# Shift, scale and gate vectors of a two-layer model: strips of columns on TensorE in place of GpSimd sums

## Chip, cores and metric

One core of a Trainium2 chip runs the whole forward pass in one launch. The metric is device time in microseconds (us) of that launch, the lower the better. The kernel before takes 1464.41 us (median of 3 runs, 1463.18 to 1467.83).

## The reference, cut to what matters

Two layers over 256 tokens of 1024 features in float32. Each layer's two sublayers are modulated by vectors that come from one conditioning vector `c` (1 x 1024) and a large matrix:

```python
def ada(c, w, b, n):
    m = jax.nn.silu(c) @ w + b
    return [t[:, None, :] for t in jnp.split(m, n, axis=-1)]
...
for i in range(DEPTH):
    sh1, sc1, g1, sh2, sc2, g2 = ada(c, ada_w[i], ada_b[i], 6)
    h = modulate(rmsnorm(x, norm_mix[i]), sh1, sc1)
    ...                       # layer 0: gMLP; layer 1: attention with its own kv shift and scale
    x = x + g1 * y
    h = modulate(rmsnorm(x, norm_ffn[i]), sh2, sc2)
    x = x + g2 * moe(...)     # 64 experts, 8 of them per token, and a shared one
```

`ada_w[i]` is 1024 x 6144 and `kv_ada_w` 1024 x 2048. So 56 MB of matrices are multiplied by one vector each, a product of one row. All other matrix products have 256 rows or the rows that the router gives an expert.

## The kernel before, in words

**Blocks.** Every weight is loaded by SP's queue in blocks of 1 MB, 128 partitions x 2048 float32, into slots of 1 MB (9 in the first and third stage, 14 in the expert stages). A block of a modulation matrix holds 256 of its columns: `w[:, k, :]` for k = 0..7 is rows 128k to 128k+127. There are 24 such blocks for each layer (`a` and `A`) and 8 for the attention's keys and values (`k`), 56 in all.

**One block's sum** (class `Sum`, lines 312 to 361). The eight parts are scaled by the silu of `c` (`cs[:, k]`, one number a partition) and added into `w[:, 0, :]`. Then `total` (line 344) adds over the partitions with two TensorE matmuls against a column of ones, and `close` adds the bias. The slot is free after `total`. There are two modes. Mode `v`: VectorE does it all, one TENSOR_SCALAR and seven SCALAR_TENSOR_TENSOR, each 128x256. Mode `q`: ScalarE scales the parts in eight ACTIVATEs, and GpSimd adds them in three TENSOR_TENSORs of 1024, 512 and 256 columns.

**Stages.** (1) The start, lines 1139 to 1199: blocks 0 to 7 of layer 0 are summed (`QUIET` names the two in mode `q`), the tokens are normalized and modulated, and the first matmul of the gMLP follows. (2) The gMLP loop, lines 1297 to 1327, 48 steps: 16 `Tok` and 16 `Feat` steps of 24 matmuls each, then 16 `Out` steps. Each step's weights are split into a high and a low float32r part three steps ahead: ScalarE copies (`high`), VectorE subtracts (`low`), and in steps 16 to 43 every fourth `low` is GpSimd's (`split`, line 488, `turns`). (3) The expert stage of layer 0, `moe` from line 609: residual, router, order of the experts, then 56 blocks of expert rows in `run`. (4) The attention loop, lines 1510 to 1546, 32 steps, whose pairs of heads pass through VectorE, ScalarE, GpSimd and TensorE. (5) The expert stage of layer 1.

**What sets the order.** From line 1214 on every engine runs its instructions in the order of the program. Into the two loops the sums are dealt out by hand. `BEGIN` and `BEGIN1` (lines 42, 49) name the step in which a block's sum begins; `lighter` (line 525) chooses its mode; and `tick` (line 508), at the end of each step, gives each engine a budget of estimated microseconds (`BUDGET`, `BUDGET1`, lines 43, 55) and issues operations from the open sums until it is spent. A sum that is done waits until its age in steps passes 2; then `finish` issues its `total`. `flush` finishes what a later stage needs. `pump`, `settle` and `rest` (lines 529 to 551, 1333) do the same around the router. Modulation blocks k5 to k7 are summed there, and A0 among the experts (line 1073).

Of the kernel before, what the change touches and what calls it, by code (L numbers as in the profile page):

```python
# [16 lines left out]
P = 128  # L17
# [15 lines left out]

QUIET = (2, 5)


# [5 lines left out]
BEGIN = [(4 + 2 * i, x) for i, x in enumerate(ITEMS) if 4 + 2 * i < 46]  # L42
BUDGET = ((1.0, 1.2, 2.5), (1.6, 1.2, 2.5), (0.6, 1.2, 2.5))

# [9 lines left out]
QUEUE1 = [x for _, x in QUEUE1] + [("s", 0)]  # L54
BUDGET1 = ((1.3, 1.2, 2.5),) * 3 + ((0.8, 0.2, 2),) + ((1.8, 1.6, 3.4),) * 2 + ((1.4, 1.5, 2.5),) * 2

# [123 lines left out]
def tile_model(ctx: ExitStack, tc: tile.TileContext, A: dict, out: bass.AP):  # L180
# [3 lines left out]
    class Ordered:  # L184


        def __init__(self, eng):
            self.eng = eng
# [42 lines left out]
    def wk(shape=(P, 512), dt=F32):  # L231
        return ps.tile(list(shape), dt, tag="wk", name=nm("wk"), bufs=4)
# [27 lines left out]
    def low(t, src, eng=None):  # L260
        (eng or V).tensor_tensor(t[:, 1], src, t[:, 0], ALU.subtract)
# [21 lines left out]
    onesf = cst.tile([P, P], F32, name="onesf")  # L283
    G.memset(onesf, 1.0)
    ident = cst.tile([P, P], F32, name="ident")
    G.affine_select(ident, onesf, [[-1, P]], ALU.is_equal, 0.0, base=0, channel_multiplier=1)
# [25 lines left out]
    class Sum:  # L312

        def __init__(self, w, biasT, at, dstT, dst=None, mode="v"):
            self.w, self.biasT, self.at, self.dstT, self.dst, self.mode = w, biasT, at, dstT, dst, mode
            self.ops = {V: [], S: [], G: []}
            o = w[:, 0, :]  # L320
            for k in range(KT):
                c = cs[:, k:k + 1]
                if mode == "q":
                    self.add(S, 0.4, lambda k=k, c=c: S.activation(w[:, k, :], w[:, k, :], AF.Copy, scale=c))
                elif k:
                    self.add(V, 0.4, lambda k=k, c=c: V.scalar_tensor_tensor(o, w[:, k, :], c, o, ALU.mult, ALU.add))
                else:
                    self.add(V, 0.4, lambda c=c: V.tensor_scalar(o, o, c, None, ALU.mult))
            for k, t in ((4, 2.3), (2, 1.2), (1, 0.7)) if mode == "q" else ():
                self.add(G, t, lambda k=k: G.tensor_tensor(w[:, 0:k, :], w[:, 0:k, :], w[:, k:2 * k, :], ALU.add))  # L330

# [6 lines left out]
        def begin(self):  # L338
            for e in (V, S, G):
                for _, f in self.ops[e]:  # L340
                    f()
                self.ops[e] = []

        def total(self, pt):

            for q in range(2):
                T.matmul(pt[:, q:q + 1], self.w[:, 0, q * P:(q + 1) * P], onesf[:, 0:1], start=True, stop=True)

# [138 lines left out]

    def split(steps, k, pool, turns=None):


        if k + LA < len(steps):
            f = steps[k + LA]
            f.h = high(f.part(), pool)
        if 0 <= k + LA - 1 < len(steps):
            f = steps[k + LA - 1]
            low(f.h, f.part(), G if turns and k % turns == turns - 1 else V)

# [7 lines left out]

    credit = {V: 0, S: 0, G: 0}

    def tick(tv, ts, tg):

        spread()  # L510
        for f in list(active):
            if not f.left(V, S, G):
                f.age = getattr(f, "age", 0) + 1
                if f.age > 2:
                    f.finish()
                    active.remove(f)
        for e, t in ((V, tv), (S, ts), (G, tg)):
            credit[e] = min(credit[e], 0) + t
            for f in active:
                while credit[e] > 0 and f.ops[e] and not (e is G and f.left(V, S)):  # L520
                    t, op = f.ops[e].pop(0)
                    op()
                    credit[e] -= t

    def lighter():

        return "q" if sum(f.left(S) for f in active) < sum(f.left(V) for f in active) + 0.1 else "v"

    def pump(*engs):

        for e in engs:
            for f in active:
                if not (e is G and f.left(V, S)):
                    for _, op in f.ops[e]:
                        op()
                    f.ops[e] = []

    def settle(n=99):

        fs = [f for f in active if not f.left(V, S, G)][:n]  # L540
        if fs:
            pt = wk((P, 2 * len(fs)))
            for i, f in enumerate(fs):
                f.total(pt[:, 2 * i:2 * i + 2])
                settled.append((f, pt[:, 2 * i:2 * i + 2]))
                active.remove(f)
# [62 lines left out]
    def moe(l, own, rw, first, rest):  # L609
# [41 lines left out]
        early = len(active)  # L651
        pump(G)
        squares(0, 2)
# [4 lines left out]
        squares(1, 3)  # L658
        rest("q")
        pump(S)  # L660
# [19 lines left out]
        for k, eng, b in ((0, V, pr), (4, G, rb)):  # L680
            eng.tensor_tensor(hT[:, k:k + 4, :], xT[:, k:k + 4, :], b.unsqueeze(1).to_broadcast([P, 4, 256]), ALU.mult)

        pump(G)


# [106 lines left out]
        for tt in range(2):  # L792
            T.matmul(pst[:, tt * P:(tt + 1) * P], slot[:, tt, :], identb, start=True, stop=True)
        shared_up(16 - SH1)
        spread()
# [5 lines left out]
        V.tensor_copy(pub, puf)  # L801
        rest(*"vqvqvq")

# [7 lines left out]
        for tt in range(2):  # L811
            V.tensor_scalar(wsel[:, tt, :], wsel[:, tt, :], wrec[:, tt:tt + 1], 2.5, ALU.mult, ALU.mult)
        pump(V, S, G)
        ready = all(f.dst is None for f in active)
# [213 lines left out]
        def run():  # L1028
# [7 lines left out]
            for b in range(nblk + 2):  # L1036
# [36 lines left out]
                while due and due[0][0] <= b:  # L1073
                    begin(due.pop(0)[1], lighter())
                tick(1.6, 1.6, 4.2)
                next(over, None)
# [62 lines left out]
    with phase("pb") as pool:  # L1139
# [25 lines left out]
        for i in range(8):  # L1165
            f = ada(0, i, load(A["wada"][0, i]), "q" if i in QUIET else "v")
            if i == 1:
                nc.sync.dma_start(xt, A["x"].rearrange("(a p) d -> p a d", p=P))
            f.begin()
            f.total(pa[:, 2 * i:2 * i + 2])  # L1170
            if i == 1:
                rt = b8((P, 2, D))
                normed(pieces(xt), rt, rstd_of(pieces(xt), rt))
                pts = transposed(rt, ("acc",) * 4)
# [20 lines left out]
        for q in range(2):  # L1195
            low(early[q], wi[0][:, 4 * q:4 * q + 4, :], G)
        V.tensor_tensor(adaT[0][:, 0:16], pa, pkc("adab0")[:, 0:16], ALU.add)
# [99 lines left out]
        for k in range(n + 16):  # L1297
            for at, x in BEGIN:
                if at == k:
                    begin(x, lighter())  # L1300
            if k in (2, 6, 10):
                fetch_bv(512 * (k + 2) // 4, 512)
            split(steps, k, pool, 4 if 16 <= k < 44 else None)
            e = k + 4 - n
# [20 lines left out]
            if k >= 42:  # L1325
                next(weighing, None)
            tick(*((0, 1.2, 0) if 17 <= k < 20 or k > 45 else BUDGET[k // 16]))
        settle()
# [4 lines left out]
    def rest(*modes):  # L1333

        for x, m in zip(list(sums), modes):
            begin(x, m)
# [300 lines left out]
```

## Time and profile before

| what | value |
|---|---|
| runs, median (lowest to highest) | 1464.41 us (1463.18 to 1467.83) |
| the profiled execution's own time | 1460.32 us |
| its span in the trace | 1458.6 us |
| TensorE matmul, busy | 1352.2 us, 93% |
| VectorE (DVE), busy | 853.3 us, 58% |
| ScalarE (ACT), busy | 537.5 us, 37% |
| GpSimd (POOL), busy | 213.9 us, 15% |
| moved by DMA | 516.59 MB, mean 354 GB/s |
| mean granted clock of TensorE | 0.961 |

The profile is one execution; its records give each instruction's start and length on its engine. PE is TensorE's matmul row, PEld its weight loads. Busy shares are averages over stages with different limits, so the prediction reads them stage by stage. "Idle before" and "waited for" name the engine whose work ended a wait. PEclk is the share of TensorE's full clock that was granted.

### The profile page before, as it was taken

How to read it: one execution, taken by the hardware profiler on the slowest of the kernel's cores; microseconds unless marked ns; L12 is line 12 of the kernel's file. 1: busy time of each engine (PE TensorE's matmuls, PEld its weight loads, DVE VectorE, ACT ScalarE, POOL GpSimd, SP SyncE). 2: the span in 40 equal slices, each digit the busy share in tenths (PEclk: the TensorE clock that was granted, in tenths of full speed). 3: DMA queues.
4: the chain of work that ended last, by engine and by line, in shares of the span. 5: the costliest groups of instructions: out<-in, count | busy, mean ns of one | idle time of the engine just before them, and what ended most of it. 6: DMA issues, size and time to landing. Idle time of an engine off the chain costs nothing. (4 is left out here: it accounts for less than half of the span.)

```text
span 1458.6 us, 27101 instructions
## 1 busy us (share of the span) xinstructions
PE 1352.2 (93%) x10782; PEld 893.6 (61%) x10782; DVE 853.3 (58%) x1568; ACT 537.5 (37%) x1143; POOL 213.9 (15%) x160
## 2 busy tenths in 40 slices
PE   4797888899999999999988988899999999999996
PEld 3797866655555555555547966775555555555553
DVE  7898897544444444444459977854444444444444
ACT  4565556222322222323236656342322223222222
POOL 4135355110000000000004644320000000000000
PEclk7799999899999999999999989999999999999998
DMA  9876767499999999999995855759999999999995
GB/s 371 323 262 230 271 224 314 173 368 418 420 419 419 419 419 419 420 418 420 419 403 210 324 178 207 286 206 390 405 419 419 420 419 419 419 419 420 419 419 216
DMA packets 72697, 516.59 MB, mean 354 GB/s; under 512 B 8308, under 2 KB 8436, under 8 KB 10358
## 3 DMA queue, kind: packets, MB, share of 16 engines
q1 hardware_dynamic: 72132, 514.03, 87.3%
q8 instruction: 86, 1.41, 0.4%
q10 hardware_dynamic: 436, 0.79, 0.2%
q14 instruction: 43, 0.35, 0.1%
HBM read 513.75 MB, written 1.05 MB: 353 GB/s over the span
## 5 line engine op out<-in xcount | busy, mean ns | idle before, releaser
L194 PE MATMUL wk<-w,b 128*32 128x256 f32 (+1 forms) x4928 | 413.2, 386 | 10.7 <-DMA w<-in_wexp_dram 10.7
L194 PEld LDWEIGHTS wk<-w,b 128*32 128x32 f32 (+1 forms) x4928 | 236.2, 122 | 153.5 <-DMA w<-in_wexp_dram 16.3
L194 DVE TENSOR_TENSOR s<-s,s 64x512 fp32r<-64x512 f32 x220 | 151.0, 686 | 125.3 <-ACT s L194 121.8
L194 PE MATMUL wk<-w,ht 128*32 128x512 f32 (+1 forms) x1232 | 212.5, 601 | 0.4 <-ACT ht L194 0.4
L194 DVE TENSOR_TENSOR s<-wk,g 128x512 f32<-128x512 f32 x110 | 76.1, 692 | 185.2 <-PE wk L194 185.2
L194 POOL TENSOR_TENSOR w<-w 128x1024 f32<-128x1024 f32 (+2 forms) x84 | 135.0, 1608 | 183.1 <-ACT w L194 179.4
L194 DVE SCALAR_TENSOR_TENSOR w<-w,cs 128x256 f32<-128x256 f32 x196 | 153.7, 785 | 5.3
L194 PE MATMUL wk<-s,b 128*128 128x256 f32 (+2 forms) x1024 | 149.4, 295 | 0.0
L194 POOL TENSOR_TENSOR t<-t,mhalf 128x2 f32<-128x2 f32 (+1 forms) x7 | 4.6, 662 | 971.7 <-DVE t L194 971.7
L194 ACT COPY ht<-wk 128x128 f32<-128x128 f32 x110 | 29.3, 266 | 312.0 <-PE wk L194 312.0
L194 ACT CAST s<-s 64x512 fp32r<-64x512 f32 x220 | 134.4, 611 | 15.2 <-DVE s L194 12.4
L194 PEld LDWEIGHTS wk<-s,b 128*128 128x128 f32 (+1 forms) x1024 | 124.7, 185 | 15.7 <-issue 1.1
L194 PE MATMUL acc<-s,h 128*128 128x512 f32 x440 | 131.6, 420 | 0.4 <-DVEq L1086 0.4
L194 ACT ACTIVATE b<-wk,adaT,sc 128x256 f32<-128x256 f32 x112 | 63.3, 565 | 180.5 <-DVE b L194 180.5
L194 DVE TENSOR_SCALAR b<-wk,sc,adaT 128x256 f32<-128x256 f32 x112 | 61.0, 544 | 100.5 <-PE wk L194 100.2
L194 ACT ACTIVATE h<-wk 64x256 f32<-64x256 f32 (+1 forms) x114 | 43.0, 378 | 195.0 <-PE wk L194 195.0
L194 PEld LDWEIGHTS wk<-w,ht 128*32 128x32 f32 (+1 forms) x1232 | 50.4, 120 | 94.3 <-issue 89.3
L194 PEld LDWEIGHTS acc<-s,h 128*128 128x128 f32 x440 | 74.0, 188 | 52.7 <-DVE s L194 35.1
L194 DVE TENSOR_TENSOR scr<-w,scr 128x1024 fp32r<-128x1024 f32 x71 | 102.5, 1449 | 5.8 <-ACT scr L194 5.7
L194 DVE SCALAR_TENSOR_TENSOR h<-wk,ws,h 64x256 f32<-64x256 f32 x110 | 54.0, 491 | 80.1 <-ACT h L194 79.3
L194 ACT CAST scr<-w 128x1024 fp32r<-128x1024 f32 x80 | 83.2, 1045 | 45.8 <-PE wk L194 23.2
L194 ACT ACTIVATE w<-w,cs 128x256 f32<-128x256 f32 x224 | 96.6, 502 | 0.9 <-DMA w<-in_wada_dram 0.8
(238 smaller groups left out, 1428.9 us busy)
## 6 DMA issues: line engine op xcount, KB each, us to landing
w<-in_wexp_dram SPq DMA_DIRECT2D x384, 1024.0 KB, 16.7
w<-in_wada_dram SPq DMA_DIRECT2D x48, 1024.0 KB, 8.0
w<-in_win_dram SPq DMA_DIRECT2D x16, 1024.0 KB, 7.1
w<-in_wqkvo_dram SPq DMA_DIRECT2D x16, 1024.0 KB, 8.6
w<-in_wout_dram SPq DMA_DIRECT2D x8, 1024.0 KB, 6.4
w<-in_wkva_dram SPq DMA_DIRECT2D x8, 1024.0 KB, 6.5
w<-in_wsh_dram SPq DMA_DIRECT2D x6, 1024.0 KB, 4.8
xt<-in_x_dram SPq DMA_DIRECT2D x1, 1024.0 KB, 10.0
```

The source lines that it names most:

```text
L194: r = f(*a, **k)
```

## The change

The mode `q` goes. In its place comes mode `p`: eight matmuls on TensorE, each with 32 equal columns of `cs[:, k]` as its stationary part, four of them side by side in strips of 32 rows of one PSUM tile, two rounds of four. ScalarE copies the tile back over `w[:, 0, :]`, and `total` uses a column of 1/32 for it. The start's eight blocks are all of mode `p`. In the loops `lighter` gives a new sum to VectorE when less than 1 us of estimated work is open there (in the gMLP loop in steps under 30 only), and otherwise to TensorE. A finished sum waits for an age over 1 in place of 2. The `low` halves that GpSimd made (two in the start, every fourth in steps 16 to 43) go to VectorE. Around the router of layer 0 the blocks k5 to k7 are summed after the expert order is sent off, in mode `p`.

```diff
-QUIET = (2, 5)
-BUDGET = ((1.0, 1.2, 2.5), (1.6, 1.2, 2.5), (0.6, 1.2, 2.5))
+BUDGET = ((1.0, 0.9, 0.9), (1.4, 0.9, 0.9), (0.1, 0.9, 0.9))
-BUDGET1 = ((1.3, 1.2, 2.5),) * 3 + ((0.8, 0.2, 2),) + ((1.8, 1.6, 3.4),) * 2 + ((1.4, 1.5, 2.5),) * 2
+BUDGET1 = ((1.5, 0.9, 0.9),) * 8
...
+    c32 = cst.tile([P, 1], F32, name="c32")
+    G.memset(c32, 1.0 / 32.0)
...
-            self.ops = {V: [], S: [], G: []}
+            self.ops = {V: [], S: [], T: []}
             o = w[:, 0, :]
+            if mode == "p":
+                self.ps = None
+                for q in range(2):
+                    self.add(T, 0.45, lambda q=q: self.four(q))
+                self.add(S, 0.4, lambda: S.copy(o, self.ps))
+                return
...
-                if mode == "q":
-                    self.add(S, 0.4, lambda k=k, c=c: S.activation(w[:, k, :], w[:, k, :], AF.Copy, scale=c))
-                elif k:
-                    self.add(V, 0.4, lambda k=k, c=c: V.scalar_tensor_tensor(o, w[:, k, :], c, o, ALU.mult, ALU.add))
+                if k:
+                    self.add(V, 0.5, lambda k=k, c=c: V.scalar_tensor_tensor(o, w[:, k, :], c, o, ALU.mult, ALU.add))
...
-            for k, t in ((4, 2.3), (2, 1.2), (1, 0.7)) if mode == "q" else ():
-                self.add(G, t, lambda k=k: G.tensor_tensor(w[:, 0:k, :], w[:, 0:k, :], w[:, k:2 * k, :], ALU.add))
+        def four(self, q):
+            if self.ps is None:
+                self.ps = wk((P, 256))
+            for j in range(4):
+                k = 4 * q + j
+                T.matmul(self.ps[32 * j:32 * j + 32, :], cs[:, k:k + 1].to_broadcast([P, 32]), self.w[:, k, :],
+                         start=(q == 0), stop=(q == 1))
...
-            low(f.h, f.part(), G if turns and k % turns == turns - 1 else V)
+            low(f.h, f.part())
...
-                if f.age > 2:
+                if f.age > 1:
...
-        for e, t in ((V, tv), (S, ts), (G, tg)):
+        for e, t in ((S, ts), (V, tv), (T, tp)):
...
-                while credit[e] > 0 and f.ops[e] and not (e is G and f.left(V, S)):
+                while credit[e] > 0 and f.ops[e] and not (e is S and f.left(T)):
...
-    def lighter():
-        return "q" if sum(f.left(S) for f in active) < sum(f.left(V) for f in active) + 0.1 else "v"
+    def lighter(v=True):
+        return "v" if v and sum(f.left(V) for f in active) < 1 else "p"
...
-        rest("q")
         pump(S)
...
-        pump(G)
...
+        pump(S)
+        while sums:
+            rest("p")
+            pump(T, S)
         shared_up(16 - SH1)
...
-        rest(*"vqvqvq")
...
-        pump(V, S, G)
...
-                tick(1.6, 1.6, 4.2)
+                tick(1.6, 0.9, 0.9)
...
-            f = ada(0, i, load(A["wada"][0, i]), "q" if i in QUIET else "v")
+            f = ada(0, i, load(A["wada"][0, i]), "p")
...
-            low(early[q], wi[0][:, 4 * q:4 * q + 4, :], G)
+            low(early[q], wi[0][:, 4 * q:4 * q + 4, :])
...
-                    begin(x, lighter())
+                    begin(x, lighter(k < 30))
...
-            split(steps, k, pool, 4 if 16 <= k < 44 else None)
+            split(steps, k, pool)
...
-            tick(*((0, 1.2, 0) if 17 <= k < 20 or k > 45 else BUDGET[k // 16]))
+            tick(*((0, 0.9, 0.9) if 17 <= k < 20 or k > 45 else BUDGET[k // 16]))
```

## Rows read from the trace of the kernel before

**Rows 1.** Stages: window, length, busy us (count) by engine, PEclk, DMA share, GB/s.

```profile
60.00:270.00 210.00, 182.06 (x1222) 166.31 (x1221) 184.59 (x287) 119.52 (x240) 96.64 (x58) 0.93 0.68 252
320.00:745.00 425.00, 419.97 (x3624) 236.98 (x3624) 197.99 (x374) 117.13 (x252) 0.00 (x0) 1.00 1.01 419
...
745.00:960.00 215.00, 187.60 (x1297) 156.52 (x1294) 177.45 (x328) 123.55 (x283) 87.93 (x72) 0.93 0.65 249
```

**Rows 2.** Timeline, VectorE and GpSimd: start, length, instructions of one kind merged.

```profile
11.70 3.48 DVE L194 SCALAR_TENSOR_TENSOR w<-w,cs 128x256 f32<-128x256 f32 x7
...
22.87 12.49 DVE L194 SCALAR_TENSOR_TENSOR w<-w,cs 128x256 f32<-128x256 f32 x8
23.03 9.57 POOL L194 TENSOR_TENSOR w<-w 128x1024 f32<-128x1024 f32 x6 [4.64 <-ACT w L194]
...
107.42 1.22 DVE L194 TENSOR_TENSOR scr<-w,scr 128x1024 fp32r<-128x1024 f32 x1
```

**Rows 3.** Timeline, end of the start: first weight block in, first gMLP matmul.

```profile
30.48 1.99 ACT L194 CAST scr<-w 128x1024 fp32r<-128x1024 f32 x2 [4.18 <-DMA w<-in_win_dram]
...
46.13 0.17 DVE L194 TENSOR_TENSOR adaT<-wk,pk 128x16 f32<-128x16 f32 x1 [1.11 <-PE wk L194]
...
47.67 22.61 PE L194 MATMUL acc<-scr,hh 128*128 128x256 f32 x163 [1.58 <-ACT h L194]
```

**Rows 4.** Timeline, TensorE among the experts: strips of 32 columns (128*32), then full width.

```profile
980.96 3.66 PE L194 MATMUL wk<-w,b 128*32 128x256 f32 x64
984.55 0.61 PE L194 MATMUL wk<-gu,s 128*128 128x8 f32 x4
```

**Rows 5.** Groups of VectorE, 47 to 235 us: xcount | busy us, mean ns | idle before.

```profile
L194 DVE TENSOR_TENSOR scr<-w,scr 128x1024 fp32r<-128x1024 f32 x39 | 58.2, 1499 | 5.7 <-ACT scr L194 5.7
L194 DVE SCALAR_TENSOR_TENSOR w<-w,cs 128x256 f32<-128x256 f32 x63 | 51.9, 825 | 1.6
```

**Rows 6.** Waits of TensorE, 47 to 233 us: total us, times, longest.

```profile
PE wk L194 <- DVE scr L194: 7.6, 1, 7.6
PE acc L194 <- POOL scr L194: 4.0, 2, 2.4
PE wk L194 <- DVE h L194: 4.0, 2, 3.2
PE wk L194 <- ACT s L194: 2.4, 1, 2.4
```

**Rows 7.** Waits of TensorE, 774 to 931 us, the three longest in total.

```profile
PE acc L194 <- ACT pm L194: 5.3, 3, 2.6
PE acc L194 <- POOL h L194: 3.6, 1, 3.6
PE wk L194 <- DVE scr L194: 3.1, 2, 2.6
```

**Rows 8.** Two stretches of the loops, columns as in Rows 1.

```profile
112.00:160.00 48.00, 37.29 (x279) 36.89 (x278) 41.18 (x47) 25.77 (x49) 22.75 (x13) 0.86 0.70 270
...
834.00:889.00 55.00, 45.16 (x313) 36.53 (x313) 44.55 (x82) 32.38 (x96) 24.60 (x22) 0.84 0.42 152
```

**Rows 9.** Timeline, layer 0's router stretch: factor copied; first expert matmul.

```profile
243.44 0.37 ACT L194 COPY h<-wk 128x256 f32<-128x256 f32 x1 [1.13 <-PE wk L194]
...
284.18 1.08 PE L194 MATMUL wk<-w,b 128*64 128x256 f32 x8
```

**Rows 10.** Timeline, the same two instructions in layer 1.

```profile
945.71 0.37 ACT L194 COPY h<-wk 128x256 f32<-128x256 f32 x1 [5.94 <-PE wk L194]
...
974.64 3.67 PE L194 MATMUL wk<-w,b 128*64 128x256 f32 x32
```

**Rows 11.** Timeline, end of the attention loop: last sums on VectorE, residual.

```profile
926.83 4.83 DVE L194 SCALAR_TENSOR_TENSOR w<-w,cs 128x256 f32<-128x256 f32 x3
...
930.66 1.95 PE L194 MATMUL wk<-onesf,ident 128*128 128x128 f32 x16
...
933.62 1.28 DVE L194 TENSOR_TENSOR s<-acc,g 128x512 f32<-128x512 f32 x2
```

More of the change, by code (lines that the diff above doesn't have):

```diff
@@ L338, in begin @@
         def begin(self):
-            for e in (V, S, G):
+            for e in (V, T, S):
                 for _, f in self.ops[e]:
@@ L346, in total @@
             for q in range(2):
-                T.matmul(pt[:, q:q + 1], self.w[:, 0, q * P:(q + 1) * P], onesf[:, 0:1], start=True, stop=True)
+                T.matmul(pt[:, q:q + 1], self.w[:, 0, q * P:(q + 1) * P], (c32 if self.mode == "p" else onesf)[:, 0:1],
+                         start=True, stop=True)
         def close(self, pt):
@@ L486, in ep, with split @@
                     self.ep_(tt, self.p[tt])
-    def split(steps, k, pool, turns=None):
+    def split(steps, k, pool):
         if k + LA < len(steps):
@@ L504, in begin, with tick @@
         active.append(kvada(x[1], w, mode) if x[0] == "k" else ada(int(x[0] == "A"), x[1], w, mode))
-    credit = {V: 0, S: 0, G: 0}
-    def tick(tv, ts, tg):
+    credit = {V: 0, S: 0, T: 0}
+    def tick(tv, ts, tp):
         spread()
         for f in list(active):
-            if not f.left(V, S, G):
+            if not f.left(V, S, T):
                 f.age = getattr(f, "age", 0) + 1
-                if f.age > 2:
+                if f.age > 1:
                     f.finish()
                     active.remove(f)
-        for e, t in ((V, tv), (S, ts), (G, tg)):
+        for e, t in ((S, ts), (V, tv), (T, tp)):
             credit[e] = min(credit[e], 0) + t
             for f in active:
-                while credit[e] > 0 and f.ops[e] and not (e is G and f.left(V, S)):
+                while credit[e] > 0 and f.ops[e] and not (e is S and f.left(T)):
                     t, op = f.ops[e].pop(0)
@@ L532, in pump @@
             for f in active:
-                if not (e is G and f.left(V, S)):
+                if not (e is S and f.left(T)):
                     for _, op in f.ops[e]:
@@ L538, in settle @@
     def settle(n=99):
-        fs = [f for f in active if not f.left(V, S, G)][:n]
+        fs = [f for f in active if not f.left(V, S, T)][:n]
         if fs:
@@ L651, in moe @@
         early = len(active)
-        pump(G)
+        pump(T, V)
         squares(0, 2)
@@ L681, in moe @@
             eng.tensor_tensor(hT[:, k:k + 4, :], xT[:, k:k + 4, :], b.unsqueeze(1).to_broadcast([P, 4, 256]), ALU.mult)
-        pump(G)
         sc = om([P, 2, NE])
```

## The prediction

> **What bounds the kernel now.** I read the stages first. Among the experts DMA moves 419 GB/s at a share of 1.01, and GpSimd does nothing [rows 1]: neither these stages nor their 425 us of stream are touched by the change, and an earlier start of them is an earlier end. The two loops are another matter: at 60 to 270 and 745 to 960 us the DMA share is 0.68 and 0.65, VectorE is busy 88% and 83%, and TensorE only 87% [rows 1]. So I look there for what TensorE waits for, and why VectorE is so full.
>
> VectorE's fullness is partly a fight with GpSimd. Seven SCALAR_TENSOR_TENSORs take 3.48 us, 0.50 each, with GpSimd idle; eight of them take 12.49 us, 1.56 each, while GpSimd adds its parts for 9.57 us beside them [rows 2]. In the gMLP loop the mean is 825 ns for 63 of them, and 1499 ns for a `low` [rows 5] that alone takes 1.22 [rows 2]. So a sum given to GpSimd delays VectorE, whose `low` halves TensorE waits for.
>
> TensorE's waits in the loops are the price. In the gMLP loop it waits 7.6 us for a `low` of VectorE, 4.0 for two of GpSimd, 4.0 for VectorE's middle step and 2.4 for ScalarE, 18.0 in all [rows 6]. In the attention loop the three longest are 5.3, 3.6 and 3.1 us [rows 7]; five smaller ones in the same view, 5.0 together, bring it to 17. After such waits the granted clock falls: it averages 0.86 and 0.84 in the worst stretches, 48 and 55 us long [rows 8]. If the rest was at the lower level, 1.2 GHz, that is 28% and 32% of the time at half speed, worth at most 7 and 9 us; idle time inside costs nothing, so I take 5 and 6.
>
> **The change part by part.** *How many sums go where.* Walking `BEGIN`, `lighter`, the budgets and `flush` step by step gives: before, 28 sums on VectorE and 28 in mode `q`; after, 17 on VectorE (6 in the gMLP loop, 10 in the attention loop, A0) and 39 in strips (8 in the start, 15 and 13 in the loops, k5 to k7). So the words "a larger part on VectorE" do not hold by count: VectorE gets fewer sums, and nine `low` halves more.
>
> *The start.* The blocks land at the rate of the DMA, and the first weight block lands at 30.48 [rows 3]; the eight modulation blocks are ahead of it in the queue, so all are in by then, the last one a block (about 2.5 us) earlier. Yet the bias add of the sums is at 46.13 and the first matmul at 47.67 [rows 3], since VectorE works off 12.49 us of slowed sums [rows 2]. In strips the last block needs 0.9 us (below; 1.8 at half clock), a copy and the total, and is done before ScalarE's two copies end at 32.5. Then VectorE's two `low` halves, new on it, 1.22 each, run from 31.5 to 33.9, and from the bias add to the first matmul it is 1.5 us as now [rows 3]: 35.4. Gain 12.3 us; 9 if TensorE is still behind with earlier blocks, 15 if the halves are put behind the bias add.
>
> *The strips.* Among the experts 64 records of strip matmuls 128*32 x 256 columns take 3.66 us [rows 4]; a float32 matmul shows as two records, so eight matmuls take 16/64 of that, 0.92 us, and 28 sums in the loops 25.6 us, all of it in TensorE's own order and on the path. The totals stay as they are. ScalarE's copy, 0.37 us as for a tile of this size [rows 9], comes a step later and replaces eight ACTIVATEs. Two waits are new. A strip waits on TensorE for its block's transfer, and every matmul queues behind it; but SP's queue loads blocks in the order of the steps, and with a third of the DMA's time free [rows 1] they should be in. ScalarE's copy waits for the strips, and behind it stand the `high` copies; those are three steps ahead, and the strips are a step old.
>
> *VectorE, GpSimd and ScalarE in the loops.* GpSimd loses all its sums and its seven `low` halves, so VectorE runs at its price alone. In the gMLP loop that is 46 `low` at 1.22 and 42 SCALAR_TENSOR_TENSORs at 0.50, 77 us, in place of 58.2 + 51.9 = 110 [rows 5], though seven more `low` are on it. Per step it is below 3.5 us, and TensorE's steps of 24 matmuls, half of x48, cost 3 us plus 0.5 to 1.1 for strips and totals. So TensorE becomes the bound in both loops, and its waits mostly go. Not all: the middle steps and the softmax of a pair are chains from engine to engine. Of the 18 + 5 + 17 + 6 = 46 us of waits and lost clock I keep a sixth, 8 us. Bounds: none kept, or half, 23. Net of strips the loops gain 46 - 8 - 25.6 = 12.4 us. The transfers don't replace the waits: slots come free earlier, since a strip sum ends in three steps where a `q` sum took six, and GpSimd's queue issues no loads.
>
> *The router of layer 0.* From the copied factor to the first expert matmul it is 40.7 us [rows 9]; in layer 1, where no sum runs on GpSimd or VectorE in that stretch, 28.9 [rows 10]. After the change layer 0 resembles layer 1, plus three strip sums, 2.8 us, whose copies stand behind ScalarE's queue, another 1 us or so, on TensorE ahead of the shared expert. The new place also frees the slots of k5 to k7 later; what then loads later are experts that wait for slots anyway. Gain 11.8 - 3.8 = 8; bounds 4 and 11.8.
>
> *The end of the attention loop.* VectorE runs slowed sums from 926.83 on and starts the residual at 933.62, a us after TensorE's last matmuls of 930.66 [rows 11], and the weight sums behind it are late too. No VectorE sum is open after step 28 now. Gain 2 us, 0 to 3. A0 goes to VectorE, which is idle half the time there: nothing, and if it were not, one sum of 4 us.
>
> *The sum.* 12.3 + 12.4 + 8 + 2 = 34.7 us. The profiled execution took 1460.3 us, 4.1 under the median of the runs. 1460.3 - 34.7 = 1425.6 on its scale; I give 1426.
>
> **The rivals.** *(a) All waits go.* TensorE, with VectorE a third emptier, never waits in the loops: 8 us more, and 4 of the 7.5 us that the upper bounds elsewhere hold, 1413. For it: the waits of rows 6 and 7 name VectorE and GpSimd, both unloaded. Against it: the chains. Chance 0.22.
>
> *(b) VectorE stays the bound.* The nine `low` halves more keep it late, and half or more of the waits stay: 46 - 30 - 25.6 = -10 in the loops, and with 22 elsewhere 1448 or later; if nearly all stay, 46 - 44 - 25.6 = -24 and 1462, no change. For it: VectorE is the fullest engine [rows 1]. Against it: 77 for 110 us. Chance 0.08.
>
> *(c) Slower.* A strip sum holds one of four `wk` tiles in PSUM until ScalarE's copy, a step later, and TensorE runs in order: where the next tile isn't free, it stops. The like of it is the wait of 2.4 us for a copy by ScalarE [rows 6]. At 2.4 us for each of 28 sums that is 67 us, 1426 + 67 = 1493; it decides above 34.7 / 28 = 1.2 us a sum. Against it: it happened once with the eight spreads of that loop, which use the same kind of tile. Chance 0.06.
>
> *(d) Changing the array's shape.* Full-width records follow the strips at 984.55, before the strips' 980.96 + 3.66 = 984.62 is over [rows 4]: no gap is seen. As a mechanism: a stop at each change into and out of strips, one strip record (64 of four at a time in 3.66 us, so 0.23 each) on each side of the two rounds of 39 sums, would cost 39 x 4 x 0.23 = 36 us at most where every round stood alone, and 18 for two changes a sum: 1426 + 18 = 1444. Chance 0.06. (The Trainium skill, TensorEngine Tiling (Array Packing), Key Properties, says that changing the tiling mode drains TensorE; by that rule it would be (d), and the trace's row doesn't show it.)
>
> **How the numbers follow.** My forecast has 0.58, (a) 0.22, (b) 0.08, (c) 0.06, (d) 0.06. I take 0.3%, 4.4 us, as what a measurement tells from no change. Faster: 0.58 + 0.22 + 0.06 + 0.03 of (b) = 0.89. The same: 0.05, the rest of (b). Slower: 0.06, (c). The range takes in (a) and (d). Its low end: with every upper bound the gain is 34.7 + 8 + 7.5 = 50 us, 1410, and if half of the strips in the loops lie in time in which TensorE waits anyhow, 12.8 us less, 1398. Its high end, 1450, is (b) with half of the waits. Outside are the rest of (b), (c), and tails.
>
> **What would show it.** First gMLP matmul near 35 us, not 47.7; `low` at a mean of 1.22 to 1.25 us and SCALAR_TENSOR_TENSOR near 0.5; TensorE's waits in the loops under 10 us together, with strip groups of 16 records in 0.9 us; factor to first expert matmul in layer 0 near 33 us; the expert stages as long as before. The prediction is wrong if TensorE waits for `wk` tiles at the strips, if the full-width matmul behind a strip starts late, if the granted clock in the loops stays at 0.85, or if the first matmul stays beyond 40 us.

## The result and the profile after

The changed kernel takes 1415.98 us (median of 4 runs, 1415.33 to 1419.82) against 1463.80 (1462.35 to 1467.83): a ratio of 0.9675, 95% interval 0.9649 to 0.970. Its profiled execution took 1416.00 us, its span 1414.2; the span of before was 1458.6, so 44.4 us are to be found in the two traces.

I cut both spans at the same events: the first and the last matmul on split weights (`scr`) of each loop, and the first and the last matmul of each expert stage on `ht`. "Router" is what lies between a loop and its expert stage, tail and residual included; some 26 us behind the expert stages are left out (the two kernels differ there by 0.2).

| us | start | gMLP loop | router 0 | experts 0 | attention loop | router 1 | experts 1 |
|---|---|---|---|---|---|---|---|
| before | 47.7 | 184.9 | 62.1 | 460.8 | 162.1 | 54.7 | 460.0 |
| after | 42.6 | 179.2 | 54.3 | 457.5 | 148.7 | 51.9 | 453.9 |
| gain | 5.1 | 5.7 | 7.8 | 3.3 | 13.4 | 2.8 | 6.1 |
| predicted | 12.3 | 12.4 with the attention loop | 8 | 0 | | 2 | 0 |

The page's busy times, and the stages of the kernel after (window, length, busy by engine with counts, granted clock, DMA share, GB/s), which answer to [rows 1]:

```profile
PE 1369.3 (97%) x11406; PEld 889.9 (63%) x11406; DVE 728.5 (52%) x1489; ACT 462.7 (33%) x958; POOL 57.4 (4%) x68
```

```profile
60.00:220.00 160.00, 160.00 (x1277) 140.91 (x1276) 102.36 (x185) 65.02 (x109) 1.82 (x2) 1.00 0.74 273
...
500.00:700.00 200.00, 199.08 (x1720) 112.45 (x1718) 95.03 (x180) 54.70 (x118) 0.00 (x0) 1.00 1.01 425
745.00:890.00 145.00, 143.54 (x1197) 120.06 (x1196) 104.45 (x219) 70.09 (x162) 24.85 (x32) 0.99 0.69 262
```

The kernel before in the first of these windows:

```profile
60.00:220.00 160.00, 141.93 (x1014) 133.88 (x1013) 146.28 (x196) 92.19 (x178) 67.95 (x39) 0.95 0.67 248
```

TensorE is busy 160.00 of 160 us in the gMLP loop at the full clock; it was 141.93 us (89%) at 0.95. VectorE has gone from 146.28 us (91%) to 102.36 (64%). And among the experts, where the change touches one sum alone (A0), DMA moves 425 GB/s in place of 419. The two groups of VectorE in the gMLP loop (count, busy us, mean ns, idle before), which answer to [rows 5]:

```profile
L192 DVE TENSOR_TENSOR scr<-w,scr 128x1024 fp32r<-128x1024 f32 x48 | 59.7, 1250 | 4.7 <-ACT scr L192 4.5
L192 DVE SCALAR_TENSOR_TENSOR w<-w,cs 128x256 f32<-128x256 f32 x42 | 20.2, 482 | 1.0
```

All waits of TensorE in the gMLP loop, then in the attention loop (total us, times, longest), which answer to [rows 6, 7]:

```profile
PE acc L192 <- DVE hh L192: 2.9, 1, 2.9
PE acc L192 <- POOL hh L192: 1.0, 1, 1.0
PE acc L192 <- DVE scr L192: 0.7, 1, 0.7
```

```profile
PE wk L192 <- POOL b L192: 0.7, 2, 0.3
PE wk L192 <- DVE b L192: 0.4, 1, 0.4
PE wk L192 <- ACT s L192: 0.2, 1, 0.2
```

The three of the first fence stand at the loop's first steps, up to 50.58 us, where the start runs out; after these TensorE does not wait once. So the loops' 35 us of waits are gone, not five sixths of them. A strip sum in the gMLP loop's own order (timeline of TensorE):

```profile
64.83 1.96 PE L192 MATMUL acc<-scr,hh 128*128 128x256 f32 x15
66.72 1.07 PE L192 MATMUL wk<-w,cs 128*32 128x256 f32 x16
67.72 1.45 PE L192 MATMUL acc<-scr,hh 128*128 128x256 f32 x10
```

Sixteen records take 1.00 us from start to start, and the full-width matmul follows with no gap: neither `wk` tiles (rival (c)) nor a change of the array's shape (rival (d)) shows. The Trainium skill, TensorEngine Tiling (Array Packing), Key Properties, has a change of tiling mode drain TensorE; no row here shows that.

The start (timeline): the small matmuls ahead of the first strips, and then its end, which answers to [rows 3]:

```profile
9.70 4.48 PE L192 MATMUL wk<-w,w 2*128 2x128 f32 x32
...
35.85 0.61 PE L192 MATMUL wk<-c,w 128*128 128x1 f32 x4 [0.49 <-ACT w L192]
...
36.38 1.79 PE L192 MATMUL wk<-w,cs 128*32 128x256 f32 x16
...
38.22 0.37 ACT L192 COPY w<-wk 128x256 f32<-128x256 f32 x1 [2.42 <-PE wk L192]
...
38.64 1.01 PE L192 MATMUL wk<-c,w 128*128 128x1 f32 x4 [0.47 <-ACT w L192]
39.69 0.17 DVE L192 TENSOR_TENSOR adaT<-wk,pk 128x16 f32<-128x16 f32 x1 [20.23 <-PE wk L192]
...
40.10 1.48 ACT L192 ACTIVATE h<-acc,adaT,scm 128x256 f32<-128x256 f32 x3 [1.51 <-DVE scm L192]
...
41.47 1.99 ACT L192 CAST scr<-w 128x1024 fp32r<-128x1024 f32 x2
...
42.57 0.58 PE L192 MATMUL acc<-scr,hh 128*128 128x256 f32 x1 [2.91 <-DVE hh L192]
```

VectorE had been idle for 20.23 us before the bias add. TensorE was not: strips, a wait of 0.48 us for ScalarE's copy, total, and only then the next block's strips, eight times. And from the bias add to the first matmul it is 2.88 us, where it was 1.54 [rows 3]: ScalarE makes the two high parts (`CAST`) behind the last sum's copy and `h`, and not ahead of them as before. From the first `COPY h` of layer 0's router to its first expert matmul it is now 33.4 us, where it was 40.7 [rows 9]:

```profile
232.16 0.37 ACT L192 COPY h<-wk 128x256 f32<-128x256 f32 x1 [4.33 <-PE wk L192]
...
265.59 1.08 PE L192 MATMUL wk<-w,b 128*64 128x256 f32 x8
```

### The profile page after: what moved, and what is told of

It is laid out like the page before. It is cut to its first block, busy times and chain, and to the rows that moved or that the text cites. A ratio compares the mean times of both kernels' runs of the same rounds, so it can differ in the third digit from the quotient of the medians.

```text
span 1414.2 us, 27956 instructions
## 1 busy us (share of the span) xinstructions
PE 1369.3 (97%) x11406; PEld 889.9 (63%) x11406; DVE 728.5 (52%) x1489; ACT 462.7 (33%) x958; POOL 57.4 (4%) x68
## 5 line engine op out<-in xcount | busy, mean ns | idle before, releaser
L192 PE MATMUL wk<-w,b 128*32 128x256 f32 (+1 forms) x4928 | 406.6, 381 | 4.9 <-DMA w<-in_wexp_dram 4.9
L192 PEld LDWEIGHTS wk<-w,b 128*32 128x32 f32 (+1 forms) x4928 | 233.0, 121 | 144.2 <-DMA w<-in_wexp_dram 8.3
L192 ACT CAST s<-s 64x512 fp32r<-64x512 f32 x220 | 134.3, 611 | 15.1 <-DVE s L192 12.4
L192 DVE TENSOR_TENSOR scr<-w,scr 128x1024 fp32r<-128x1024 f32 x80 | 99.3, 1248 | 4.8 <-ACT scr L192 4.5
L192 PEld LDWEIGHTS wk<-ident,h 64*128 64x128 f32 (+1 forms) x226 | 22.5, 137 | 92.9 <-issue 84.4
L192 PE MATMUL wk<-hh,scr 128*128 128x256 f32 x576 | 73.8, 285 | 0.0
L192 PEld LDWEIGHTS wk<-hh,scr 128*128 128x128 f32 x576 | 70.2, 191 | 3.3 <-issue 3.3
L192 DVE SCALAR_TENSOR_TENSOR w<-w,cs 128x256 f32<-128x256 f32 x119 | 58.6, 493 | 2.9
```

What stands on the lines that cost most here:

```text
L192: r = f(*a, **k)
```

## The experiments

Three things were open: which part of the change emptied the loops, whether the expert stages were shortened by the change, and what holds the start. The stages of all runs, each of one profiled execution, cut as above (times: median, lowest to highest, number of runs):

| run | us | start | gMLP loop | router 0 | experts 0 | attention loop | router 1 | experts 1 |
|---|---|---|---|---|---|---|---|---|
| e1 before | 1463.8 (1) | 50.3 | 184.8 | 64.8 | 461.1 | 162.1 | 53.6 | 459.0 |
| e2 after | 1417.6 (1) | 42.6 | 179.2 | 54.3 | 457.8 | 151.7 | 50.3 | 453.7 |
| e3 GpSimd sums | 1437.6 (1436.0 to 1439.7, 4) | 40.7 | 166.3 | 64.0 | 458.4 | 152.2 | 73.2 | 453.2 |
| e4 all strips | 1437.5 (1435.0 to 1438.2, 4) | 47.3 | 186.3 | 54.2 | 456.2 | 160.0 | 50.6 | 453.2 |
| e5 and GpSimd lows | 1445.8 (1) | 45.1 | 178.4 | 61.1 | 458.8 | 150.3 | 71.4 | 452.8 |
| e6 slots moved back | 1430.5 (1426.8 to 1432.2, 4) | 42.9 | 179.2 | 54.3 | 463.3 | 146.9 | 50.6 | 459.9 |
| e7 own slots aligned | 1417.8 (1416.5 to 1419.3, 4) | 47.8 | 179.1 | 54.3 | 457.5 | 148.6 | 50.5 | 453.6 |
| e8 start mix | 1417.8 (1417.0 to 1418.6, 2) | 43.8 | 178.1 | 54.3 | 457.2 | 148.5 | 51.8 | 455.1 |
| e9 GpSimd early | 1414.3 (1408.2 to 1419.1, 4) | 44.9 | 174.3 | 52.6 | 456.0 | 147.1 | 50.5 | 453.3 |
| e10 more VectorE | 1416.6 (1414.3 to 1419.5, 4) | 46.1 | 177.7 | 52.6 | 457.8 | 151.3 | 51.9 | 454.0 |
| e11 totals late | 1407.1 (1404.7 to 1408.3, 4) | 35.9 | 179.2 | 54.1 | 455.6 | 146.9 | 50.6 | 452.9 |
| e12 e9 and e11 | 1403.8 (1399.9 to 1410.8, 6) | 37.3 | 175.8 | 55.3 | 457.4 | 147.2 | 50.5 | 453.9 |

The start holds the same instructions in after and in e2 to e7, e9 and e10 (one memset more in e6 and e7), and yet lasts 40.7 to 47.8 us; the attention loop, where its code is that of after, lasts 146.9 to 151.7. So I read stages, and totals only where they differ by more.

### Both kernels again, on one chip (e1, e2)

No edit.

> The kernel before once more, beside the changed one on the same chip. Open: the two expert stages were 3.3 and 6.3 us shorter after the change (9.6 of the 44.3 us of the span), with DMA at 424 to 426 GB/s in place of 419 to 420. Theory A (the chip or the execution has its own DMA rate, the change has no part in it): the two kernels, profiled one after the other on one chip, move the same GB/s in the expert stages to within 1, and the stages are equal to within 2 us each; the difference of the spans falls to about 35 us. Theory B (the change does it): 5 GB/s and 9 to 10 us apart again.

> The changed kernel beside the kernel before. Theory A (chip or execution): expert stages at the rate of the kernel before in this same call, spans about 35 us apart. Theory B (the change): 424 to 426 GB/s here against 419 to 420 there, spans 43 to 46 us apart.

The spans are 46.3 us apart (1462.1 and 1415.8), the expert stages 3.3 and 5.3 us. The same window of the expert stage, 500 to 700 us, in e1:

```profile
500.00:700.00 200.00, 196.11 (x1705) 110.46 (x1700) 94.02 (x178) 55.44 (x119) 0.00 (x0) 1.00 1.01 419
```

and in e2:

```profile
500.00:700.00 200.00, 198.95 (x1722) 112.60 (x1720) 94.82 (x180) 54.73 (x119) 0.00 (x0) 1.00 1.01 426
```

Theory B: the change does it, by some way that has nothing to do with sums. GpSimd is idle in both windows.

### GpSimd sums in place of the loops' strips (e3)

```diff
-        return "v" if v and sum(f.left(V) for f in active) < 1 else "p"
+        return "v" if v and sum(f.left(V) for f in active) < 1 else "q"
```

with the old mode `q` put back beside `p`, ScalarE's budget at 1.2 and GpSimd's at 2.5.

> The changed kernel with the 28 strip sums of the loops given back to ScalarE (eight scalings) and GpSimd (three additions); the start and the router keep their strips, VectorE keeps its 17 sums and all lows. Theory A (GpSimd beside VectorE is what cost the loops): VectorE's low goes back to 1.4 us or more on the mean and its SCALAR_TENSOR_TENSOR to 0.7 or more, TensorE waits again for VectorE and GpSimd in both loops, the clock falls there, and although 28 strip sums of about 1 us leave TensorE the loops lose the 17.8 us that they won or more: 1430 to 1440. Rival (the new dealing, budgets and ages, or the start, did it, and strips only cost): TensorE saves 28 us less a few us of waits, 1390 to 1400.

The total fell to theory A's range, and for the wrong reason. In the gMLP loop the rival was right: 12.9 us less than after, with GpSimd adding all along. VectorE did slow down (its groups in that loop):

```profile
L192 DVE TENSOR_TENSOR scr<-w,scr 128x1024 fp32r<-128x1024 f32 x48 | 65.2, 1365 | 3.8 <-ACT scr L192 3.6
L192 DVE SCALAR_TENSOR_TENSOR w<-w,cs 128x256 f32<-128x256 f32 x42 | 27.0, 643 | 1.0
```

but six sums and the lows leave it room for that. What was lost was lost behind the loops: router 0 is 9.7 us longer, router 1 21.3. The timeline of e3 in router 0:

```profile
213.66 8.94 POOL L192 TENSOR_TENSOR w<-w 128x1024 f32<-128x1024 f32 x6 [6.96 <-ACT w L192]
222.56 0.71 POOL L192 TENSOR_TENSOR t<-t,mhalf 128x2 f32<-128x2 f32 x1
...
223.32 1.22 PE L192 MATMUL wk<-ident,t 128*128 128x128 f32 x4 [8.09 <-POOL t L192]
```

Two sums still open at the loop's end put 8.94 us of additions ahead of the 0.71 us that makes the norm's factor, and TensorE waits 8.09 us for it; in router 1 nine additions hold it for 13.55 us. In the attention loop 13 strip sums less bought nothing (152.2 against 148.7): there GpSimd's sums cost about what the strips do. The kernel before had such sums too, and its router 1 took 54.7 us with no wait for GpSimd; its budget gave GpSimd up to 3.4 us a step in that loop, where e3 gives 2.5. So the loss behind the loops belongs to the way e3 deals its sums out, and not to every GpSimd sum.

### Strips for VectorE's sums too (e4)

```diff
-        return "v" if v and sum(f.left(V) for f in active) < 1 else "p"
+        return "p"
```

> The changed kernel with the 17 VectorE sums (6 in the gMLP loop, 10 in the attention loop, one among the experts) made in strips as well. Theory A (in the loops TensorE is the only bound, and a strip sum costs it its own length, 16 records in 1.0 us): 16 to 17 us more, 1432 to 1433, no waits, clock 1.0. Rival 1 (strips go partly into time in which TensorE waits, or VectorE's sums still hold TensorE up here and there): under 8 us more, below 1424. Rival 2 (a change of the array's shape drains it beyond the listed length, or wk tiles run short): 2 us or more a sum, above 1448.

1437.5, some 5 us above theory A's figure, and the stages say why. The gMLP loop is 7.1 us longer for 6 sums, the attention loop 11.3 for 10 (8.3 to 13.1, with the spread of that loop): 1.2 and 1.1 a sum. TensorE waits hardly more than in after (1.9 us against 1.3 in the attention loop), and both rivals fall. Another 4.7 us are the start of this execution, whose code is unchanged. There the strips and totals run at 1.93 and 1.01 us to the end:

```profile
37.55 1.93 PE L192 MATMUL wk<-w,cs 128*32 128x256 f32 x16
39.97 1.01 PE L192 MATMUL wk<-c,w 128*128 128x1 f32 x4 [0.49 <-ACT w L192]
40.91 1.93 PE L192 MATMUL wk<-w,cs 128*32 128x256 f32 x16
```

where after had totals of 0.61 for five of its eight blocks, and strips of 1.07 for most of these. From 30 to 45 us the granted clock is 0.52 here and 0.72 there: the lower of the two levels (1.2 and 2.4 GHz) nearly throughout, against 56% of the time (1 - 0.56/2 = 0.72).

### GpSimd's lows on top of GpSimd's sums (e5)

```diff
-            low(f.h, f.part())
+            low(f.h, f.part(), G if turns and k % turns == turns - 1 else V)
...
-            split(steps, k, pool)
+            split(steps, k, pool, 4 if 16 <= k < 44 else None)
```

on e3.

> GpSimd sums in the loops as in the run before (where the gMLP loop took 166.3 us, 13 less than in the changed kernel, with no wait in TensorE's records until the router), and now also every fourth low of steps 16 to 43 on GpSimd, as in the kernel before. It asks which part of the change took TensorE's 18 us of waits out of the gMLP loop. Theory A (the seven lows on GpSimd: they stand in its queue behind additions, TensorE and VectorE wait for them): waits of 8 us or more come back, some of them named after GpSimd's scr, and the gMLP loop takes 175 to 182 us. Rival (the dealing: fewer sums on VectorE than the kernel before had there): the loop stays at 166 to 169 us.

Theory A: 178.4 us, 12.1 more than e3. GpSimd's seven lows take 2.5 us each, and VectorE's own get slower still (groups of GpSimd and VectorE, gMLP loop of e5):

```profile
L192 POOL TENSOR_TENSOR scr<-w,scr 128x1024 fp32r<-128x1024 f32 x7 | 17.7, 2534 | 0.0
```

```profile
L192 DVE TENSOR_TENSOR scr<-w,scr 128x1024 fp32r<-128x1024 f32 x41 | 63.8, 1562 | 5.4 <-ACT scr L192 5.3
```

TensorE's waits there, of which e3 had 1.8, 1.0 and none:

```profile
PE wk L192 <- DVE adaT L192: 6.8, 3, 4.1
...
PE wk L192 <- DVE h L192: 2.1, 1, 2.1
PE wk L192 <- DVE scr L192: 1.8, 1, 1.8
```

None is named after GpSimd, as I had expected of some: it delays VectorE, and TensorE waits for that. Past the first step the waits come to 11.1 us against 4.8 in e3, whose loop was not free of waits as the expectation has it: there 2.0 more were for a sum of GpSimd. The other half of the 12.1 us is the clock. Over this loop it was 0.94 here and 0.99 in e3, and the same matmuls keep TensorE busy for 166.6 us in place of 159.8. With the lows moved to VectorE and the new dealing of sums, the gMLP loop needed no strips; the 6.5 us from 184.9 to 178.4 are left to the dealing (6 VectorE sums in that loop, where there were 9 [rows 5]) and the budgets.

### Where the slots lie (e6, e7)

```diff
+    spare = cst.tile([P, 1], F32, name="spare")
+    G.memset(spare, 0.0)
```

in e6, behind `c32`; in e7 the same of 40 columns in the pool `sb`, which lies between the two pools of slots.

> The changed kernel with one spare column of float32 beside c32. The tile c32 of the change moved every tile behind it by 32 bytes: the nine slots of the weight pool from address 30432 to 30464 in a partition (a multiple of 256), the five slots of the experts' own pool from 172352 to 172384. The spare column moves them on by 32 again, to 30496 and 172416, which are 32 and 0 past a multiple of 64, as in the kernel before. Theory A (the faster transfers of the changed kernel come from where its slots lie): consecutive 1 MB loads land 2.49 us apart as in the kernel before, in place of 2.44 and 2.47, DMA moves 419 to 420 GB/s among the experts, the two expert stages are 8 to 10 us longer together and the start 0.5 us: 1425 to 1427. Rival (it comes from the work, fewer instructions on GpSimd or another order of loads): no change, 1416.

> The changed kernel with a spare tile of 160 bytes ahead of the experts' own pool, so that its five slots also begin at a multiple of 256 (172544 in place of 172384). Theory A (a slot's address sets the price of a load into it, and the two groups of intervals in the changed kernel, 2.43 to 2.45 and 2.46 to 2.48 us, are the two pools): all loads land 2.43 to 2.45 us apart, 429 to 431 GB/s, some 3 to 4 us less in each expert stage, 1408 to 1410. Rival (the own slots' address does not matter, or nothing about addresses does): 1416.

In e6 the stages are 5.8 and 6.0 us longer than in after, and the rest is within its spread:

```profile
500.00:700.00 200.00, 196.93 (x1702) 111.88 (x1696) 93.16 (x178) 55.17 (x118) 0.00 (x0) 0.99 1.01 420
```

Loads of 1 MB that follow each other land 2.49 us apart on the mean, as in the kernel before (2.49), and 2.45 in after. So a column of four bytes, `c32`, made the stream faster by where it put what lies behind it. The total, 1430.5, is above the expected 1427: the profiled execution was the fastest of the four, and what the other three lost more no trace shows.

e7 went the other way from its theory A: with the experts' own slots at multiples of 256 too, the two stages stay at 457.5 and 453.6, and the total at 1417.8. Landings are then 2.45 us apart on the mean, as in after. So the five need not lie at a multiple of 256. What is left is the weight pool's nine slots or what lies between; no run moves the nine alone, so this is likely and not shown.

The Trainium skill, DMA: Bandwidth & Descriptors, How a descriptor splits into AXI transactions, says that a transaction must start at a multiple of 256 bytes, and that where a descriptor doesn't, the bytes ahead of it are fetched too and cost beats of 32 bytes. By that page a row of 8192 bytes would cost 0.4% more at 32 past such a multiple, as the weight pool lies in e6, and 2.7% more at 224 past, as it lay before; these are estimates. The trace agrees in the direction only: both landed 2.49 us apart in place of 2.45, 1.6%. The page speaks of bytes fetched, and here the slot is written to, so it may be another effect.

### The start (e8, e11)

```diff
-            f = ada(0, i, load(A["wada"][0, i]), "p")
+            f = ada(0, i, load(A["wada"][0, i]), "v" if i in MIX else "p")
```

in e8, with `MIX = (0, 2, 4, 6)`.

> The changed kernel with blocks 0, 2, 4 and 6 of the start summed on VectorE and the other four in strips. Theory A (the start is held by TensorE's chain of strips, copy by ScalarE and total, 3.4 us a sum at half clock and 2.1 at full clock, while VectorE is idle): TensorE has four sums in place of eight, VectorE's four take about 4 us each while blocks land 2.4 us apart, the bias add follows the last block at 33 to 35 us in place of 39.7 and the first gMLP matmul comes at 35 to 38 us in place of 42.6: 1409 to 1412. Rival (the lows, the h chain and the weight blocks set it): 41 us or later, no gain.

The rival's figure, 43.8, but not for its reason (the strips' chain still ended last). TensorE's timeline near the end, weight loads among it:

```profile
35.45 1.06 PE L193 MATMUL wk<-w,cs 128*32 128x256 f32 x2
36.44 0.93 PEld L193 LDWEIGHTS wk<-onesf,w 128*128 128x128 f32 x4 [0.81 <-DVE w L193]
36.44 1.01 PE L193 MATMUL wk<-onesf,w 128*128 128x1 f32 x4
37.38 1.93 PE L193 MATMUL wk<-w,cs 128*32 128x256 f32 x14
```

The first two of block 7's strips run, then the total of block 6, whose weight load waited 0.81 us for VectorE's sum, then the other fourteen: TensorE takes things in order, and a late VectorE sum in front holds the strips behind it as the copy did.

Its start is not to be judged against the 42.6 us of after alone. The small matmuls ahead of the first strips took 4.48 us in after, and 7.19 us here and in e7 and e10, whose starts lasted 47.8 and 46.1 us. So one execution doesn't tell whether the mix gains in the start; the total shows no gain. In e7:

```profile
10.38 7.19 PE L192 MATMUL wk<-w,w 2*128 2x128 f32 x32
17.50 1.94 PE L192 MATMUL wk<-w,cs 128*32 128x256 f32 x16
```

```diff
             f.begin()
-            f.total(pa[:, 2 * i:2 * i + 2])
+            if i:
+                g.total(pa[:, 2 * i - 2:2 * i])
+            g = f
...
+        f.total(pa[:, 14:16])
```

in e11, with TensorE's order held as written and the transposes after block 2.

> The changed kernel with the start's totals one block behind: TensorE makes the strips of block i + 1 before the total of block i, in an order held as written, and the token transposes after block 2's strips. Nothing else changes. Theory A (the start is TensorE's serial chain of strips, 0.48 us of waiting for ScalarE's copy, and total, eight times): TensorE no longer waits for the copy except at the last block, a sum takes 1.6 us at full clock or 2.9 at half, and the first gMLP matmul comes 3 to 5 us earlier at the same clock: 37 to 40 us where the clock is as in the changed kernel (42.6 there), 43 to 44 where it stays at half for the whole start (47.3 and 47.8 in two such runs): 1411 to 1413. Rival (blocks' landings or ScalarE and VectorE behind the bias add hold it): 42 us or later at the same clock, 1416.

Better than theory A: 35.9 us, and 1407.1 us in all, every run below every run of the changed kernel. The timeline of e11:

```profile
28.39 1.07 PE L192 MATMUL wk<-w,cs 128*32 128x256 f32 x16 [0.82 <-DMA w<-in_wada_dram]
...
30.83 1.07 PE L192 MATMUL wk<-w,cs 128*32 128x256 f32 x16 [0.83 <-DMA w<-in_wada_dram]
31.83 1.16 PE L192 MATMUL wk<-c,w 128*128 128x1 f32 x8
...
33.03 0.17 DVE L192 TENSOR_TENSOR adaT<-wk,pk 128x16 f32<-128x16 f32 x1 [12.03 <-PE wk L192]
...
35.90 0.58 PE L192 MATMUL acc<-scr,hh 128*128 128x256 f32 x1 [2.91 <-ACT scr L192]
```

Now TensorE waits for the last two blocks' transfers, as the prediction had it. The granted clock is 0.89 from 15 to 30 us, where after had 0.62; TensorE was busy 14.18 us of these, where after had 13.05. So two things came together, the waits left out (in after eight of 0.48 us, 3.9 in all) and the higher clock; how much of the 6.7 us is whose, one profile doesn't tell. The order held as written and the later transposes are part of this edit too, and no run has them alone.

### More for VectorE or GpSimd (e9, e10), and the best version (e12)

```diff
-                    begin(x, lighter(k < 30))
+                    begin(x, lighter(k < 30) if k >= 32 or lighter() == "v" else "q")
```

in e9, with mode `q` as in e3.

> The changed kernel with the seven strip sums that begin before step 32 of the gMLP loop given to ScalarE and GpSimd (the other eight of that loop, and all later ones, stay strips; VectorE keeps its sums and all lows). With all 15 given back the gMLP loop fell from 179.2 to 166.3 us, but the router and the attention loop's tail lost 10 and 21 us, with TensorE waiting 8.1 and 13.6 us for the small GpSimd result t behind GpSimd's last additions. Theory A (a strip sum costs TensorE about a microsecond of a loop that it bounds, a GpSimd sum costs nothing there while VectorE has room, and the losses came from sums still open at the loops' ends): gMLP loop 171 to 173 us, all other stages as in the changed kernel, 1407 to 1411. Rival (GpSimd additions cost VectorE, and so TensorE, what the strips cost): gMLP loop 178 to 182, 1414 to 1419.

```diff
-BUDGET = ((1.0, 0.9, 0.9), (1.4, 0.9, 0.9), (0.1, 0.9, 0.9))
+BUDGET = ((1.3, 0.9, 0.9), (2.0, 0.9, 0.9), (0.6, 0.9, 0.9))
...
-                    begin(x, lighter(k < 30))
+                    begin(x, lighter(k < 38))
```

in e10.

> The changed kernel with VectorE's budgets in the gMLP loop raised from 1.0, 1.4, 0.1 to 1.3, 2.0, 0.6 and VectorE allowed to begin sums up to step 38: ten VectorE sums there in place of six, eleven strips in place of fifteen. Theory A (VectorE, busy 109 of 160 us in that loop, has room for 15 us more): gMLP loop 175 to 176 us, 1411 to 1413. Rival (in the steps after 30 the three VectorE operations of a middle step wait behind sums, TensorE waits for them): gMLP loop 179 or longer, 1416 or later.

e9's loop is 174.3 us: 4.9 less for seven sums, between the two theories. A wait of 2.0 us is what is missing:

```profile
PE wk L192 <- POOL w L192: 2.0, 1, 2.0
```

Its total, 1408.2 to 1419.1, can't be told from after's. e10's loop is 1.5 us shorter for four sums; TensorE waits 1.4 us for the middle steps (`h`), as its rival had it in part, and the total is the same.

> The two edits that shortened a stage, together: totals one block behind in the start (first gMLP matmul at 35.9 us in place of 42.6), and the seven early sums of the gMLP loop on ScalarE and GpSimd (gMLP loop 174.3 us in place of 179.2). Theory A (each works on its own stage): start near 36 us, gMLP loop 174 to 175, all else as in the run with late totals alone (1407.1): 1402 us. Rival (with an earlier start the loop waits for its blocks' transfers or for GpSimd's additions, so one gain eats the other): gMLP loop 178 us or longer, 1407 or later.

e12 is e9 with the start of e11. Start and loop come at 37.3 and 175.8 us, near theory A, and that start had small matmuls of 7.19 us, as the 47.8 and 46.1 us of e7 and e10 had; 1403.8 us, a ratio to the kernel before of 0.9584 (0.9557 to 0.9611), where e11 alone has 0.9623 (0.9597 to 0.9649). Against e11 the intervals overlap: the late totals are shown to help, the seven GpSimd sums on top of them only by their stage.

## Why the prediction came out right, point by point

The forecast of 1426 was 10 us too high, its range (1398 to 1450) held, and the sign was right. But only some of its terms were right.

**The start: the failed step.** "In strips the last block needs 0.9 us (below; 1.8 at half clock), a copy and the total, and is done before ScalarE's two copies end": for one block yes, 1.07 + 0.48 + 0.61. I priced the last block alone; all eight stand in one chain on TensorE, behind the small matmuls that end at 14.18, at 2.1 to 3.4 us a sum. Nor were ScalarE's two copies done at 32.5: they run from 41.47, and the 1.5 us from the bias add to the first matmul became 2.88. So the first matmul came at 42.6 and not at 35.4 (at 40.7 or later in all nine executions of this start), and the gain of 5.1 lies under my lower bound of 9 "if TensorE is still behind with earlier blocks". The named mark (beyond 40 us) showed it. e11 shows the step was feasible with another order: 35.9.

**The strips' price: right.** 0.92 us a sum was forecast; the trace has 1.00 from start to start, e4 1.1 to 1.2, with a lower clock at the beginning of its gMLP loop in it. It is on the path, as said.

**The waits: mis-sized.** I kept 8 of 46 us of waits and lost clock; TensorE keeps 1.3 in the attention loop and none in the gMLP loop past its first steps, at a clock of 0.99 to 1.00. That is the mechanism of rival (a), and the loops gained 19.1 in place of 12.4.

**What emptied the loops: right that GpSimd delays VectorE, wrong that its sums made the waits.** "A sum given to GpSimd delays VectorE, whose `low` halves TensorE waits for" [rows 2, 5]: the delay is there in e3 (643 ns for 482), the wait for a `low` is not. In the gMLP loop the seven lows on GpSimd (12.1 us, e5, beside GpSimd's sums) and the dealing and budgets (6.5) made the loss, and its 15 strip sums gave back 12.9 us of what taking these away won. So in that loop the strips, the heart of the change, cost time (e9: 4.9 us for seven of them, with nothing lost behind the loop). What won the 13.4 us of the attention loop is open: with GpSimd's sums (e3) it is 9.9 us shorter than before, but leaves nine additions to the router. The GpSimd sums did harm where I had not looked: open at a loop's end (e3).

**Router of layer 0: right.** 7.8 us against 8, to a first expert matmul after 33.4 us (33 forecast); no run takes this stretch apart. **End of the attention loop:** 2.8 against 2.

**"The expert stages as long as before": wrong.** They are 9.4 us shorter, by the place of the slots. With the slots moved back (e6) the kernel takes 1430.5, which is 33 us less than before; I had summed 34.7 for what the change is about. So the forecast was 10 us too high by the place of the slots, and that the rest of it comes out is luck: 7 us too much for the start and 7 too little for the loops cancel.

## What to carry to other kernels

Price a piece of work that moves to an in-order engine as a chain over all its pieces, with the round trip to the engine that copies its result, and put the next piece's work ahead of the wait: here the start became 6.7 us shorter by that (e11), a higher clock included. When an engine has slack, look at what stands in its queue ahead of something urgent (lows, the norm's factor) before moving the bulk of its work onto the bound engine. And when a stage without any edited work changes its length, compare the addresses of its buffers.

## What the runs showed of the hardware that I had not expected

- A shift of 32 bytes in a partition moved the stream of 1 MB loads between 419 to 420 and 425 to 426 GB/s (before, after, e1, e2, e6). Which tile's address does it, and which multiple it wants, is open: e7 shows only that the experts' own five slots need not lie at a multiple of 256.
- The same start ran in 40.7 to 47.8 us in nine executions, with a granted clock from 30 to 45 us of 0.72 in after (42.6) and 0.52 in e4 (47.3). The figure can mislead there. In e7 (47.8) the profile gives 1.00 from 15 to 30 us, though its strips take 1.94 us at 17.50, the length of the lower level; a known matmul's length tells more:

```profile
15.00:30.00 15.00, 13.85 (x87) 8.96 (x85) 1.63 (x7) 4.50 (x11) 0.70 (x1) 1.00 1.01 426
```

- A block's strips, copy and total take 3.4 us at the lower level and 2.1 at the full one.
- Strips of 32 columns between full-width matmuls cost their own 1.00 us and no gap.
